# w_ada dot products spread differently over the weight chunks of the down products

## The chip, the core and the metric

The kernel runs on one core of a Trainium2 chip. The metric is the device time of one execution in microseconds. Before the change three runs took 2405.26, 2408.19 and 2410.62 us (median 2408.19). The core has a matmul engine (PE, with its weight loads shown as PEld), a vector engine (DVE), a scalar engine (ACT), GpSimd (POOL), and a queue on SyncE (SP) from which nearly all transfers are issued, one after the other.

## What is computed

Two layers of a streaming encoder over 512 positions and 1024 channels, in f32. Each layer is SwiGLU, mixer (two attentions, a pooling branch, a merge), SwiGLU. Every one of these three has a norm in front, and a shift, a scale and a gate that come from one vector `c`:

```python
c_act = jax.nn.silu(c)
for l in range(DEPTH):
    mod = (c_act @ w_ada[l] + b_ada[l]).reshape(B, N_MOD, D_MODEL)      # N_MOD = 9
    h = modulate(rms_norm(x, norm_gain[l, 0]), mod[:, 0], mod[:, 1])
    x = x + 0.5 * mod[:, 2][:, None, :] * swiglu(h, ffn_w_gate[l, 0], ffn_w_up[l, 0], ffn_w_down[l, 0])
    h = modulate(rms_norm(x, norm_gain[l, 1]), mod[:, 3], mod[:, 4])
    x = x + mod[:, 5][:, None, :] * hybrid_mixer(h, ...)
    h = modulate(rms_norm(x, norm_gain[l, 2]), mod[:, 6], mod[:, 7])
    x = x + 0.5 * mod[:, 8][:, None, :] * swiglu(h, ffn_w_gate[l, 1], ffn_w_up[l, 1], ffn_w_down[l, 1])
```

where `swiglu(h)` is `(silu(h @ w_gate) * (h @ w_up)) @ w_down`, 1024 to 2816 to 1024 channels. `c_act @ w_ada` is a product of one row with 75 MB of weights: 2 layers x 9 modulation rows x 8 blocks of 128 channels = 144 blocks of 512 KB.

## The kernel before

Channels lie on the partitions, so a modulation row is eight columns of 128 numbers. Each of the 144 blocks of `w_ada` is one *mod step* (`mod_step`, L200): one transfer of 512 KB (L203), one dot product with the broadcast `silu(c)` on DVE (L206), and for some rows a small operation behind it (L215, L217). The first 16 are done at the start. The other 128 stand in a list in the order in which they are needed (`mod_queue`), and `mod_pop` does the next one.

Who pops? `side_work` is called at every weight chunk (`wchunk`, L262): it adds `MOD_RATE[0]` to a credit and pops one step for each whole credit. And `mod_need(l, j)` pops whatever is still missing up to row `j` of layer `l`, all at once, at the place where a row must be complete.

A matmul weight chunk of 512 KB is loaded into one of two `raw` buffers (L266), split by ACT into a rounded high part `whi` (L277) and by DVE into the rest `wlo` (L279), and each product is three matmuls (L119 to L121: high x high, high x low, low x high). `whi` and `wlo` have three buffers each. In a down product, chunks arrive in a fixed order, and the last two of a pass are held and used together, one output tile after the other.

A SwiGLU (`Ffn.run`) works in three parts: 6, 8 and 8 tiles of 128 hidden channels. A part makes its tiles (gate and up), then multiplies them with their rows of `w_down` in two passes of 512 output channels. In part 0 the gate and up products are plain, in parts 1 and 2 they come from `seven` (L507), which makes two tiles at a time from seven half-size products, and `MOD_RATE` is 0 there. Part 0 also makes the operands for `seven` (`Blocks`) bit by bit on DVE and ACT.

The mod steps of a SwiGLU load into the four `v2` buffers. `seven` and `Blocks` use the same four: a mod transfer waits in the SP queue until its buffer is free, and everything behind it in that queue waits with it. In the last part's down products the norm of the next stage takes the `v2` or `b` buffers (`prefetch`), and the mod steps stop (`mod_tag` becomes "raw"). `prefetch` of a mixer first calls `mod_need(l, 5)`, ahead of the last part's first weight chunk. In the second half of a mixer 24 mod steps are done from `b` buffers, one a chunk.

The order of the instructions on each engine and in the SP queue is set at build time: a scheduler places them by its own estimate of when each could run, so transfers, dot products and splits may change places against the order of the code.

Of the kernel before, what the change touches and what calls it, by code (L numbers as in the profile page):

```python
# [40 lines left out]
def encoder_kernel(tc, xT, c, w_ada, b_ada, gains, w_gate, w_up, w_down, w_qkv, w_f, w_ubg,  # L41
# [28 lines left out]
    def mmt(shape=(P, T)):  # L70
        return ps.tile(list(shape), F32, tag="mm", bufs=4, name=nm("mm"))
# [17 lines left out]
    class Task:  # L89
# [3 lines left out]
        def run(self):  # L93
            fn, self.fn = self.fn, None
            if fn is not None:
                fn()

    def later(delay, fn, group=None):
        t = Task(pe[0] + delay, fn, group)
        tasks.append(t)  # L100
        return t
# [129 lines left out]
    def mod_need(l, j):  # L231
        while mod_ptr[0] < min(len(mod_queue), (l * 9 + j + 1) * 8 - 16):
            mod_pop()

    MOD_RATE = [1.0]
# [66 lines left out]
    def xd(d):  # L302
        return x_blocks[d // 2][:, d % 2, :]
# [84 lines left out]
    def k_outer(chunk_src, nch, lhs_rhs, before_last=None):  # L388

        if before_last is None:
            parts, nheld = [(None, slice(0, T), [acc() for _ in range(4)])], 2
        else:
            parts = [(hs, slice(hs * HALF, (hs + 1) * HALF), [b((P, HALF)) for _ in range(4)])
                     for hs, b in enumerate((mmt, acc))]
            nheld = 3

        def go(part, j, chunks):
            _, cols, accs = part  # L400
            for c, hi, lo in chunks:
                for kk in range(2):
                    a, b, x, y = lhs_rhs(hi[:, kk, :], lo[:, kk, :], 2 * c + kk, j)
                    triple(accs[j], a, b, x[:, cols], y[:, cols], start=(c == 0 and kk == 0),
                           stop=(c == nch - 1 and kk == 1))

        held = []
        for c in range(nch):
            if before_last is not None:
                if c == nch - 2:  # L410
                    quiet[0] = 8
                    before_last()
                quiet[0] = 8
            hi, lo = wchunk(chunk_src(c), (2, T))
            if c < nch - nheld:
                for part in parts:
                    for j in range(4):
                        go(part, j, [(c, hi, lo)])
            else:
                held.append((c, hi, lo))  # L420
        if before_last is not None:
            quiet[0] = 5
        for part in parts:
            for j in range(4):
                go(part, j, held[:-2])
            for j in range(4):
                go(part, j, held[-2:])
                yield j, part[0], part[2][j]

    def residual_tail(d, hs, acc_j, gate, nxt):  # L430

        cols = slice(0, T) if hs is None else slice(hs * HALF, (hs + 1) * HALF)
        x = xd(d)[:, cols]
        nc.vector.scalar_tensor_tensor(x, acc_j, gate, x, op0=ALU.mult, op1=ALU.add)  # L434
        if nxt is not None:
            nxt.norm.sq(d, hs)
            if d == KD - 1 and hs == 0:
                later(FRONT, lambda: nxt.norm.front(0, mmt))
                later(BACK, lambda: nxt.norm.back_start(0, mmt))
# [113 lines left out]
    def apply(parts, func, **kw):  # L553

        o = t1(T)
        n = T // len(parts)
        for i, p in enumerate(parts):
            nc.scalar.activation(o[:, i * n:(i + 1) * n], p, func, **kw)
        return o


    class Ffn:
# [32 lines left out]
        def run(self, nxt):  # L595
            l, s, ms = self.l, self.s, self.ms
            in_ffn[0] = True
            mod_tag[0] = "v2"
            parts = ((0, 6), (6, 8), (14, 8))
            for part, (f0, nf) in enumerate(parts):  # L600
                acts = []
                n = 0
                if part == 0 and self.norm is None:
                    acts = self.start()
                    n = 3
                    blocks = Blocks()
                elif part == 0:
                    g0, u0, g1 = self.pre
                    pg, pu, pg1 = mmt(), mmt(), mmt()
                    for hs in range(2):  # L610
                        self.norm.back(hs, acc if hs else mmt)
                        cols = slice(hs * HALF, (hs + 1) * HALF)
                        if hs == 0:
                            later(FRONT1, lambda: self.norm.front(1, acc))
                            later(BACK1, lambda: self.norm.back(1, acc))
                        for k in range(KD):
                            self.unit(pg, g0, cols, (k,))
                            self.unit(pu, u0, cols, (k,))
                        self.unit(pg1, g1, cols)
                    u1 = self.gate_up(1, 1)  # L620
                    acts.append(self.act(0, pg, pu))
                    pu1 = mmt()
                    self.unit(pu1, u1)
                    acts.append(self.act(1, pg1, pu1))
                    n = 2
                    blocks = Blocks(self.norm.xa, modc[:, l, 3 * ms])
                if part == 0:
                    blocks.schedule(T_FIRST, T_STEP)
                elif part == 1:
                    blocks.finish()  # L630
                MOD_RATE[0] = 0.0 if part else 1.0
                while part and n < nf:
                    both = [apply(p, AF.Silu)
                            for p in seven([w_gate[l, s, f0 + n + i] for i in range(2)], blocks, acc)]
                    ups = seven([w_up[l, s, f0 + n + i] for i in range(2)], blocks, mmt)
                    for i, sg in enumerate(both):
                        acts.append(self.act(n + i, None, ups[i], sg))
                    n += 2
                while n < nf:
                    g = self.gate_up(0, f0 + n)  # L640
                    u = self.gate_up(1, f0 + n)
                    pg, pu = mmt(), mmt()
                    self.unit(pg, g)
                    self.unit(pu, u)
                    acts.append(self.act(n, pg, pu))
                    n += 1
                mod_need(l, 3 * ms + 2)
                MOD_RATE[0] = 1.0
                for c0 in (0, T):
                    def src(c):  # L650
                        r0 = (f0 + 2 * c) * P
                        return w_down[l, s, r0:r0 + 2 * P, c0:c0 + T].rearrange("(k p) c -> p k c", p=P)

                    def ops(hi, lo, kt, j):
                        return (hi[:, j * P:(j + 1) * P], lo[:, j * P:(j + 1) * P],
                                acts[kt][:, 0, :], acts[kt][:, 1, :])

                    last = part == len(parts) - 1
                    if last and c0 == 0 and nxt is not None:
                        nxt.prefetch("v2")  # L660
                        mod_tag[0] = "raw"
                    split = last and c0 > 0
                    hook = None
                    if split:
                        hook = nxt.prefetch_weights if nxt is not None else (lambda: None)
                    for j, hs, o in k_outer(src, nf // 2, ops, hook):
                        d = c0 // P + j
                        residual_tail(d, hs, o, modc[:, l, 3 * ms + 2, d:d + 1], nxt if last else None)
                        if last and nxt is None:
                            cols = slice(0, T) if hs is None else slice(hs * HALF, (hs + 1) * HALF)  # L670
                            nc.sync.dma_start(out[:, d, cols], xd(d)[:, cols])
# [590 lines left out]
```

## Time and profile before

| what | us |
|---|---|
| median of 3 runs | 2408.19 |
| the profiled execution, its own time | 2409.17 |
| its span, first to last instruction | 2407.4 |
| first SwiGLU of layer 0 (`l, s` = 0, 0) | 0 to 371 |
| mixer of layer 0 | 371 to 861 |
| second SwiGLU of layer 0 (0, 1) | 861 to 1210 |
| first SwiGLU of layer 1 (1, 0) | 1210 to 1559 |
| mixer of layer 1 | 1559 to 2051 |
| second SwiGLU of layer 1 (1, 1) | 2051 to 2407 |

Matmuls are shown with a modelled duration and overlap, so the steady pace of a 128x512 matmul is read from start to start, not from its mean. Within the first SwiGLU, by the matmul lines: the down products of part 0 run from 92.6 to 125.3, those of part 1 from 205.4 to 249.0, and those of part 2 from 328.9 to 371.

The views used are the engines' busy time, the table by stretches of time with the clock granted to PE, the list of waits, the timeline of one engine, and the transfers with their time to landing.

### The profile page before, as it was taken

The page shows a single profiled execution, that of the slowest core. Times are in us where ns is not written, and L with a number is a line of the kernel's source. Part 1 is how long each engine was busy: PE and PEld are TensorE (multiplying, and loading weights), DVE is VectorE, ACT ScalarE, POOL GpSimd, SP SyncE. Part 2 cuts the span into 40 slices and gives each one's busy share as a digit, 9 for nine tenths or more (in the row PEclk, how much of TensorE's full clock was granted, in tenths as well). Part 3 has the DMA queues.
Part 4 walks back from the last instruction along what each step waited for, and adds up shares of the span by engine and source line. Part 5 has one row for each costly group of instructions (what it writes and reads, how often), then busy time and mean ns, then how long its engine had stood idle before and what let it go on. Part 6 is the DMA issues. An engine that isn't in the chain of part 4 may idle for free. (4 is left out here: it accounts for less than half of the span.)

```text
span 2407.4 us, 36815 instructions
## 1 busy us (share of the span) xinstructions
PE 2361.9 (98%) x14106; PEld 2086.8 (87%) x14106; DVE 1728.9 (72%) x3070; ACT 1197.8 (50%) x2090; POOL 351.7 (15%) x423
## 2 busy tenths in 40 slices
PE   7999999999999999999999999999999999999999
PEld 5898988778878898989998989888788788989898
DVE  8987886787665476878577868777866755658583
ACT  5353545786632353535543636466765324536352
POOL 3000011144432210000100000112444322000000
PEclk9999999999999999999999999999999999999999
DMA  7534362323345524343325343623233554223322
GB/s 274 201 106 175 106 219 88 93 79 107 109 171 200 175 99 156 108 165 105 132 87 185 105 165 104 215 83 102 74 120 104 198 182 168 71 97 106 101 95 103
DMA packets 116436, 320.93 MB, mean 133 GB/s; under 512 B 11138, under 2 KB 13314, under 8 KB 116260
## 3 DMA queue, kind: packets, MB, share of 16 engines
q1 hardware_dynamic: 115106, 314.38, 38.8%
q0 software_dynamic: 1152, 4.19, 0.5%
q8 instruction: 111, 1.82, 0.3%
q14 instruction: 65, 0.53, 0.1%
q10 hardware_dynamic: 2, 0.00, 0.0%
HBM read 312.16 MB, written 6.38 MB: 132 GB/s over the span
## 5 line engine op out<-in xcount | busy, mean ns | idle before, releaser
L277 ACT CAST whi<-raw 128x1024 fp32r<-128x1024 f32 (+1 forms) x267 | 277.5, 1043 | 449.6 <-PE acc L120 251.7
L279 DVE TENSOR_TENSOR wlo<-raw,whi 128x1024 fp32r<-128x1024 f32 x259 | 321.1, 1242 | 168.2 <-ACT whi L277 165.0
L119 PE MATMUL acc<-b,whi 128*128 128x512 f32 (+1 forms) x960 | 361.8, 377 | 3.8 <-ACT whi L277 3.8
L121 PE MATMUL acc<-b,wlo 128*128 128x512 f32 (+1 forms) x960 | 358.0, 373 | 0.6 <-DVE wlo L279 0.6
L120 PE MATMUL acc<-b,whi 128*128 128x512 f32 (+1 forms) x960 | 358.5, 373 | 0.0
L119 PEld LDWEIGHTS acc<-b,whi 128*128 128x128 f32 x960 | 181.4, 189 | 36.0 <-ACT whi L277 4.6
L121 PEld LDWEIGHTS acc<-b,wlo 128*128 128x128 f32 x960 | 181.7, 189 | 33.1 <-DVE wlo L279 1.5
L120 PEld LDWEIGHTS acc<-b,whi 128*128 128x128 f32 x960 | 181.8, 189 | 30.1
L119 PE MATMUL acc<-hhi,whi 128*128 128x512 f32 x480 | 191.3, 400 | 7.2 <-DVE b L1051 3.1
L120 PE MATMUL acc<-hlo,whi 128*128 128x512 f32 x480 | 188.0, 392 | 1.1 <-DVE hlo L711 1.1
L121 PE MATMUL acc<-hhi,wlo 128*128 128x512 f32 x480 | 187.7, 392 | 0.3 <-DVE wlo L279 0.3
L385 DVE TENSOR_TENSOR ptb<-v,ptb 128x1024 fp32r<-128x1024 f32 x128 | 156.5, 1223 | 36.4 <-ACT ptb L384 36.2
L384 ACT CAST ptb<-v 128x1024 fp32r<-128x1024 f32 x128 | 134.1, 1050 | 92.8 <-DVE v L452 47.9
L384 ACT CAST whi<-raw 128x1024 fp32r<-128x1024 f32 (+1 forms) x128 | 106.7, 833 | 99.3 <-PE acc L120 56.2
L119 PE MATMUL acc<-whi,hhi 128*128 128x512 f32 x336 | 137.8, 411 | 0.9 <-DVE xv L385 0.9
L206 DVE CUSTOM_DVE_ANT_0 v<-v,b,badac 128x1024 f32<-128x1024 f32 x96 | 127.2, 1333 | 12.3 <-DMA v<-in_w_ada_dram 12.0
L121 PE MATMUL acc<-whi,hlo 128*128 128x512 f32 x336 | 131.9, 393 | 0.0
L120 PE MATMUL acc<-wlo,hhi 128*128 128x512 f32 x336 | 131.7, 392 | 0.0
L385 DVE TENSOR_TENSOR wlo<-raw,whi 128x1024 fp32r<-128x1024 f32 (+1 forms) x128 | 121.7, 950 | 6.4 <-ACT whi L384 4.6
L434 DVE SCALAR_TENSOR_TENSOR xv<-acc,modc,xv 128x512 f32<-128x512 f32 (+1 forms) x112 | 77.2, 690 | 64.1 <-PE acc L121 64.1
L119 PEld LDWEIGHTS acc<-hhi,whi 128*128 128x128 f32 x480 | 90.7, 189 | 26.1 <-DVE b L1051 4.0
L329 POOL TENSOR_TENSOR ssum<-ssum,t 128x256 f32<-128x256 f32 (+1 forms) x45 | 46.9, 1043 | 442.4 <-ACT t L328 442.2
(315 smaller groups left out, 6664.5 us busy)
## 6 DMA issues: line engine op xcount, KB each, us to landing
v<-in_w_ada_dram SPq DMA_DIRECT2D x96, 512.0 KB, 5.0
raw<-in_w_down_dram SPq DMA_DIRECT2D x88, 512.0 KB, 3.7
raw<-in_w_up_dram SPq DMA_DIRECT2D x82, 512.0 KB, 3.6
raw<-in_w_gate_dram SPq DMA_DIRECT2D x79, 512.0 KB, 3.6
raw<-in_w_ubg_dram SPq DMA_DIRECT2D x56, 512.0 KB, 3.5
b<-in_w_ada_dram SPq DMA_DIRECT2D x48, 512.0 KB, 4.7
raw<-in_w_qkv_dram SPq DMA_DIRECT2D x42, 512.0 KB, 3.8
raw<-in_w_branch_dram SPq DMA_DIRECT2D x24, 512.0 KB, 3.7
```

The costliest lines, as they stand in the source:

```text
L119: mm(o, lh, rh, start=start, stop=False)
L120: mm(o, lh, rl, start=False, stop=False)
L121: mm(o, ll, rh, start=False, stop=stop)
L206: dot = nc.vector.tensor_tensor_reduce(out=raw, in0=raw, in1=silc[0], scale=1.0, scalar=badac[:, l, j, d:d + 1], op0=ALU.mult, op1=ALU.add ...
L277: nc.scalar.copy(hi, raw)
L279: lo_eng.tensor_tensor(lo, raw, hi.bitcast(F32), op=ALU.subtract)
L329: nc.gpsimd.tensor_tensor(self.ssum[:, cols], self.ssum[:, cols], q, op=ALU.add)
L384: nc.scalar.copy(hi, src)
L385: nc.vector.tensor_tensor(lo, src, hi.bitcast(F32), op=ALU.subtract)
L434: nc.vector.scalar_tensor_tensor(x, acc_j, gate, x, op0=ALU.mult, op1=ALU.add)
```

## The change

One number that was 1.0 for the down products of every part becomes 1.9, 1.2, 1.5 or 1.2, by layer and SwiGLU:

```diff
@@ -645,7 +645,7 @@
                     acts.append(self.act(n, pg, pu))
                     n += 1
                 mod_need(l, 3 * ms + 2)
-                MOD_RATE[0] = 1.0
+                MOD_RATE[0] = (1.9, 1.2, 1.5, 1.2)[2 * l + s]
                 for c0 in (0, T):
                     def src(c):
                         r0 = (f0 + 2 * c) * P
```

The mod steps are the same 128, in the same order; they are popped elsewhere. Steps by place, counted in the order in which the two programs pop them:

| place | before | changed |
|---|---|---|
| SwiGLU (0, 0), part 0, down, 6 chunks | 6 | 11 |
| SwiGLU (0, 0), part 1, down, 8 chunks | 8 | 15 |
| SwiGLU (0, 0), part 2, in one go by `mod_need(0, 5)` | 10 | 0 |
| SwiGLU (0, 1), down of parts 0 and 1 | 6 and 8 | 7 and 10 |
| SwiGLU (1, 0), part 0, in one go by `mod_need(1, 2)` | 2 | 0 |
| SwiGLU (1, 0), down of parts 0 and 1 | 6 and 8 | 9 and 12 |
| SwiGLU (1, 0), part 2, in one go by `mod_need(1, 5)` | 10 | 0 |
| SwiGLU (1, 1) | 0 | 0 |

The plain gate and up chunks of part 0 and the mixers keep their counts (the mixer of layer 0 does steps that stand two places later in the list).

First place: the SP queue at the start of the down products of part 2 of SwiGLU (0, 0). `raw` from `in_w_down_dram` are weight chunks, `v` from `in_w_ada_dram` mod steps, `b` from `in_w_qkv_dram` weights loaded ahead for the mixer. Before, the end of the nine steps ahead of the third chunk, and what follows:

```order
L203 DMA v2_502_3323<-in_w_ada_dram 128x1024
L203 DMA v2_503_3327<-in_w_ada_dram 128x1024
L203 DMA v2_504_3331<-in_w_ada_dram 128x1024
L266 DMA raw_517_3404<-in_w_down_dram 128x2x512
L203 DMA v2_505_3335<-in_w_ada_dram 128x1024
L266 DMA raw_520_3410<-in_w_down_dram 128x2x512
L266 DMA b_542_3552<-in_w_qkv_dram 128x2x512
L266 DMA raw_536_3492<-in_w_down_dram 128x2x512
```

Changed, from the first chunk on:

```order
L266 DMA raw_513_3350<-in_w_down_dram 128x2x512
L266 DMA raw_516_3380<-in_w_down_dram 128x2x512
L266 DMA raw_519_3410<-in_w_down_dram 128x2x512
L266 DMA raw_522_3416<-in_w_down_dram 128x2x512
L266 DMA b_544_3558<-in_w_qkv_dram 128x2x512
L266 DMA raw_538_3498<-in_w_down_dram 128x2x512
```

The third and fourth chunk now follow the first two with no mod step ahead of them.

Second place: DVE near the end of the down products of part 0 of the same SwiGLU. Rows `wlo` are splits of weight chunks (of the fourth, fifth and sixth chunk before; of the fifth and sixth in the changed program), `L206 ISA v` dot products, `xv` the residual sums of finished output tiles. Before:

```order
L279 TENSOR_TENSOR wlo_880<-raw_877,whi_879 128x1024
L434 TENSOR_SCALAR xv_78<-acc_753,modc,xv_78 128x512
L385 TENSOR_TENSOR b_884<-v_155_775,b_883 128x1024
L206 ISA v_176_911,modc<-v_176_911,b_73,badac 128x1024
L206 ISA modc 128x1
L434 TENSOR_SCALAR xv_78<-acc_754,modc,xv_78 128x512
L206 ISA v_180_920,modc<-v_180_920,b_73,badac 128x1024
L206 ISA modc 128x1
L434 TENSOR_SCALAR xv_85<-acc_755,modc,xv_85 128x512
L279 TENSOR_TENSOR wlo_917<-raw_914,whi_916 128x1024
L434 TENSOR_SCALAR xv_85<-acc_756,modc,xv_85 128x512
L279 TENSOR_TENSOR wlo_926<-raw_923,whi_925 128x1024
```

Changed, from the last residual sum on (three dot products stand between the fourth chunk's split and this piece already):

```order
L434 TENSOR_SCALAR xv_85<-acc_756,modc,xv_85 128x512
L206 ISA v_180_923,modc<-v_180_923,b_73,badac 128x1024
L206 ISA modc 128x1
L279 TENSOR_TENSOR wlo_930<-raw_927,whi_929 128x1024
L215 TENSOR_SCALAR apre<-modc,gainc 128x1
L206 ISA v_184_933,modc<-v_184_933,b_73,badac 128x1024
L206 ISA modc 128x1
L206 ISA v_185_937,modc<-v_185_937,b_73,badac 128x1024
L206 ISA modc 128x1
L215 TENSOR_SCALAR apre<-modc,gainc 128x1
L279 TENSOR_TENSOR wlo_944<-raw_941,whi_943 128x1024
```

Two dot products moved in between the splits of the fifth and the sixth chunk, which stood a single residual sum apart.

Third place: PE where it first uses that sixth chunk (`whi_182`, `wlo_183` before; `whi_187`, `wlo_188` changed). Before:

```order
L119 MATMUL acc_166_870<-b_128_657,whi_182_925 128x512
L120 MATMUL acc_166_870<-b_128_657,whi_182_925 128x512
L121 MATMUL acc_166_870<-b_128_657,wlo_183_926 128x512
L119 MATMUL acc_166_870<-b_144_742,whi_182_925 128x512
L120 MATMUL acc_166_870<-b_144_742,whi_182_925 128x512
L121 MATMUL acc_166_870<-b_144_742,wlo_183_926 128x512
```

Changed:

```order
L119 MATMUL acc_168_876<-b_128_657,whi_187_943 128x512
L120 MATMUL acc_168_876<-b_128_657,whi_187_943 128x512
L119 MATMUL acc_169_877<-b_98_493,whi_182_929 128x512
L120 MATMUL acc_169_877<-b_98_493,whi_182_929 128x512
L121 MATMUL acc_168_876<-b_128_657,wlo_188_944 128x512
L119 MATMUL acc_168_876<-b_144_742,whi_187_943 128x512
```

Two matmuls of the next output tile moved ahead of the first one that needs the sixth chunk's low part.

## The prediction, made before the changed kernel ran

> **What bounds the kernel now.** I read the engines' busy time first, then the table by stretches of time, then the idle gaps of PE with what ended them.
>
> ```profile
> PE 2361.9 (98%) x14106; PEld 2086.8 (87%) x14106; DVE 1728.9 (72%) x3070; ACT 1197.8 (50%) x2090; POOL 351.7 (15%) x423
> ```
>
> PE is busy for 98% of the span. The change takes no matmul away, so it can only gain where PE stands still or runs slowly, and can only lose by making PE wait. By stage (columns: length, then busy time of PE, PEld, DVE, ACT and POOL, granted clock, DMA share, GB/s):
>
> ```profile
> 0.00:371.00 371.00, 352.37 (x2216) 316.69 (x2217) 305.62 (x458) 179.28 (x277) 26.81 (x24) 1.00 0.52 178
> 861.00:1210.00 349.00, 349.00 (x2346) 323.56 (x2345) 260.41 (x408) 168.56 (x269) 9.30 (x9) 1.00 0.37 127
> 1210.00:1559.00 349.00, 346.37 (x2304) 319.70 (x2304) 273.75 (x430) 166.77 (x266) 10.74 (x11) 1.00 0.45 148
> ```
>
> SwiGLU (0, 1) has no idle PE time at all: there the new rate can gain nothing. SwiGLU (1, 0) has 349.00 - 346.37 = 2.63 us. In SwiGLU (0, 0) most of the idle time lies in the start, which the change leaves alone. The rest is in one place, and PE's timeline shows it together with that of (1, 0) (start, duration, what, and in brackets the idle time before and what ended it):
>
> ```profile
> 341.36 0.50 PE L119 MATMUL acc<-b,whi 128*128 128x512 f32 x1 [1.44 <-ACT whi L277]
> 342.62 0.50 PE L121 MATMUL acc<-b,wlo 128*128 128x512 f32 x1 [0.30 <-DVE wlo L279]
> ...
> 1529.63 0.50 PE L119 MATMUL acc<-b,whi 128*128 128x512 f32 x1 [2.33 <-ACT whi L277]
> 1530.89 0.74 PE L121 MATMUL acc<-b,wlo 128*128 128x512 f32 x1 [0.30 <-DVE wlo L279]
> ```
>
> Both stand at the third weight chunk of a last part's down products. Who made `whi` late is seen on ACT and in the SP queue:
>
> ```profile
> 318.10 15.54 SPq L203 DMA_DIRECT2D v<-in_w_ada_dram  x9
> 333.69 0.43 SPq L266 DMA_DIRECT2D raw<-in_w_down_dram  x1
> 340.26 1.04 ACT L277 CAST whi<-raw 128x1024 fp32r<-128x1024 f32 x1 [8.25 <-DMA raw<-in_w_down_dram]
> ...
> 1505.49 15.49 SPq L203 DMA_DIRECT2D v<-in_w_ada_dram  x9
> 1521.04 0.43 SPq L266 DMA_DIRECT2D raw<-in_w_down_dram  x1
> 1528.53 1.04 ACT L277 CAST whi<-raw 128x1024 fp32r<-128x1024 f32 x1 [9.17 <-DMA raw<-in_w_down_dram]
> ```
>
> Nine mod transfers occupy the queue for 15.5 us, since each waits for a `v2` buffer that a dot product must free, and the third chunk stands behind them. ACT had been idle for 8.25 and 9.17 us when it came. So the transfer, not ACT, is what is late.
>
> The gaps also cost something behind them. The same table in steps of 3.41 us:
>
> ```profile
> 339.72:343.14 3.42, 1.68 (x6) 0.97 (x6) 2.46 (x6) 1.28 (x2) 0.00 (x0) 1.00 0.95 373
> 343.14:346.55 3.41, 3.41 (x9) 2.67 (x9) 3.19 (x5) 1.86 (x2) 0.00 (x0) 0.50 0.75 247
> 1527.56:1530.97 3.41, 1.04 (x4) 0.57 (x4) 2.40 (x6) 1.04 (x1) 0.00 (x0) 1.00 0.82 317
> 1530.97:1534.39 3.42, 3.42 (x8) 2.67 (x9) 3.38 (x5) 2.09 (x2) 0.00 (x0) 0.50 0.64 196
> ...
> 1882.55:1885.96 3.41, 1.84 (x9) 1.25 (x8) 2.74 (x6) 2.14 (x4) 0.30 (x1) 1.00 0.00 0
> 1885.96:1889.40 3.44, 3.44 (x17) 2.83 (x16) 3.15 (x5) 0.51 (x1) 1.42 (x1) 1.00 0.39 141
> ```
>
> After each stall PE works through one step at a granted clock of 0.50, with 8 or 9 matmuls instead of 17. Idle times of 1.74 and 2.38 us within a step (3.42 - 1.68, 3.42 - 1.04) were followed by the half clock, 1.57 us (3.41 - 1.84) was not. One such step costs 3.41 x 0.5 = 1.71 us.
>
> **The change part by part.**
>
> *The two bursts of ten disappear.* The third chunk then follows the second in the SP queue and arrives with time to spare; next to be late would be the later chunks, which wait only for a `raw` buffer, as they do now without a stall. Gain: 1.44 + 0.30 + 1.71 = 3.45 us in (0, 0) and 2.33 + 0.30 + 1.71 = 4.34 us in (1, 0), together 7.79 us.
>
> [...]
>
> *The burst of two in (1, 0), part 0, disappears.* No PE wait stands at it; nothing is gained.
>
> *The dot products themselves* are the same 128. DVE and ACT gain or lose no work, only its place counts.
>
> *Part 0 of SwiGLU (0, 0): 11 steps instead of 6, among six chunks.* This stretch and its neighbours are the tightest, since DVE also makes operands for `seven`:
>
> ```profile
> 78.00:92.60 14.60, 14.60 (x66) 12.11 (x65) 13.72 (x21) 4.10 (x5) 0.00 (x0) 1.00 0.73 249
> 205.40:249.00 43.60, 43.60 (x195) 36.09 (x194) 27.69 (x41) 11.13 (x12) 0.00 (x0) 1.00 0.39 141
> ```
>
> Just ahead of it DVE works 94% of the time. The DVE rows that give each kind's price, from start to start:
>
> ```profile
> 85.77 1.28 DVE L206 CUSTOM_DVE_ANT_0 v<-v,b,badac 128x1024 f32<-128x1024 f32 x1
> 86.98 1.28 DVE L206 CUSTOM_DVE_ANT_0 v<-v,b,badac 128x1024 f32<-128x1024 f32 x1
> ...
> 97.82 1.22 DVE L385 TENSOR_TENSOR b<-v,b 128x1024 fp32r<-128x1024 f32 x1
> 98.95 0.68 DVE L452 TENSOR_TENSOR v<-v,v 128x512 f32<-128x512 f32 x1
> ...
> 108.73 1.23 DVE L279 TENSOR_TENSOR wlo<-raw,whi 128x1024 fp32r<-128x1024 f32 x1 [0.62 <-ACT whi L277]
> 109.87 0.74 DVE L434 SCALAR_TENSOR_TENSOR xv<-acc,modc,xv 128x512 f32<-128x512 f32 x1
> 110.54 1.21 DVE L279 TENSOR_TENSOR wlo<-raw,whi 128x1024 fp32r<-128x1024 f32 x1
> ```
>
> A dot product takes 1.21 us, a split 1.14 (L279) or 1.13 (L385), a residual sum 0.67, and I give L452 the same 0.67. From 98.95 to the end of the sixth chunk's split stand 3 dot products, 2 L452, 4 residual sums, one L385, 3 splits and small operations (0.2, my estimate): 3.63 + 1.34 + 2.68 + 1.13 + 3.42 + 0.2 = 12.4, so 111.4; the trace has 110.54 + 1.21 = 111.75, which bears the method out. The changed program has 8 dot products there: 18.45, so 117.4 if DVE never waits. When is that split needed?
>
> ```profile
> 114.43 0.39 PE L119 MATMUL acc<-b,whi 128*128 128x512 f32 x1
> 115.79 0.39 PE L119 MATMUL acc<-b,whi 128*128 128x512 f32 x1
> 116.25 0.39 PE L121 MATMUL acc<-b,wlo 128*128 128x512 f32 x1
> ```
>
> The sixth chunk's low part is first read at 116.25; a matmul takes (115.79 - 114.43) / 6 = 0.23 us, and two of them now stand ahead, so at 116.70. The old margin of 4.5 us becomes a lateness of 117.4 - 116.7 = 0.7 us at least. It is more if DVE has to wait for mod transfers, since eight dot products use four buffers twice. Their time from issue to landing, in three stretches (the last is a weight chunk among mod transfers):
>
> ```profile
> v<-in_w_ada_dram SPq DMA_DIRECT2D x2, 512.0 KB, 4.1
> v<-in_w_ada_dram SPq DMA_DIRECT2D x3, 512.0 KB, 5.3
> raw<-in_w_down_dram SPq DMA_DIRECT2D x2, 512.0 KB, 5.8
> ```
>
> With 4.1 us they arrive almost in step with DVE and the split is 0.8 us late; following the chain of buffer, transfer and dot product with 5.5 us it is 2.4 us late, with 6 us 3.8 us late. I take 1.7 us, between the first two, since the queue here is fuller than in the stretch that has 4.1. Ends: 0 (the order of arrival is kinder) and 3.8.
>
> *What follows it.* `seven` starts behind, and its second `raw` buffer is freed by the same late split:
>
> ```profile
> 115.99 0.69 DVE L515 TENSOR_TENSOR v<-raw 128x512 f32<-128x512 f32 x1 [4.25 <-DMA raw<-in_w_gate_dram]
> 120.80 1.23 DVE L385 TENSOR_TENSOR ptb<-v,ptb 128x1024 fp32r<-128x1024 f32 x1 [0.39 <-ACT ptb L384]
> ...
> 128.42 0.28 PE L130 MATMUL acc<-b,ptb 128*128 128x256 f32 x1
> ```
>
> Its first sum is ready 128.42 - 122.03 = 6.4 us early. The split ends 5.65 us later (117.4 for 111.75) and PE itself 0.7: 6.4 - 5.65 + 0.7 = 1.4 us remain. No cost; up to 1 us if the transfer lands late.
>
> *Part 1 of SwiGLU (0, 0): 15 instead of 8.* DVE is busy 27.69 of 43.60 us; seven more make 27.69 + 7 x 1.21 = 36.2, 83%. Where nine transfers held a chunk back by 15.5 us, now at most six stand ahead of one: about 15.54 / 9 x 6 = 10.4 us, 5.2 less than at the bursts, whose chunk was 1.44 and 2.33 us late. So it is some 3 us early. No cost.
>
> *SwiGLUs (0, 1) and (1, 0).* One to four more steps a part, 1.2 to 4.8 us of DVE time in 32.7 (6 chunks) or 43.6 us, where DVE stands at 260.41 / 349 = 75% and 78% on average and PE never waits in the parts concerned. No cost.
>
> *Sum.* 2409.17 (the profiled execution) - 7.79 + 1.7 = 2403.1. The median is 2408.19, 0.98 lower: **2402.1 us**.
>
> **The rivals.**
>
> 1. *No new wait in part 0.* If DVE has the split ready by 116.7, the whole gain stays: 2408.19 - 7.79 = 2400.4. For it: two matmuls were moved ahead to cover the split. Against: 0.7 us are missing even without a wait for a transfer.
>
> 2. *The new wait halves the clock.* If more than about 1.65 us of it fall into one step of 3.41 us (between the 1.57 and 1.74 above), 1.71 us are added. With 2.4 to 3.8 us of wait: 2400.4 + 2.4 + 1.7 = 2404.5 to 2400.4 + 3.8 + 1.7 = 2405.9. Landing times over 5.5 us decide it; the 5.8 us row speaks for it, the 4.1 row against.
>
> 3. *Slower: the mod transfers hold chunks back in every pass.* With two steps at a chunk, the SP queue gets two mod transfers ahead of each chunk. If a `v2` buffer came free more slowly than every 2.7 us (two in a chunk's 43.60 / 8 = 5.45 us), each of the four passes of parts 0 and 1 of SwiGLU (0, 0) would end in a stall like the bursts', 3.45 to 4.34 us: 2400.4 + 13.8 = 2414.2 to 2400.4 + 17.4 = 2417.8. For it: DVE's 94% ahead of part 0. Against: in the bursts one came free every 15.54 / 9 = 1.73 us.
>
> 4. *Half the gain is not there.* If the half clock were not due to the gaps, 4.37 - 1.7 = 2.7 us are gained: 2405.5. For it: the step after the 1.57 us kept its clock, so idle time does not always bring it. Against: twice out of twice over 1.74 us. [...]
>
> 5. *Nothing is gained at the former bursts*, because the third or a later chunk now waits for something else, say the weights loaded ahead for the mixer (`b` from `in_w_qkv_dram`), which share the queue: about 2408. For it: the DMA share of 0.95 in the stretch 339.72 to 343.14. Against: ten transfers fewer compete there.
>
> **How the numbers follow.** Forecast 0.50 (its own range 2400.5 to 2404), rival 1 0.13, rival 2 0.16, rival 3 0.10, rival 4 0.03, rival 5 0.08. A difference of 0.2%, 4.8 us, is about what a measurement of this kernel can tell from no change: faster is below 2403.4, slower above 2413.0. Faster: 0.42 of the forecast and rival 1, 0.55. Slower: rival 3 and a little of the others, 0.11. The same: 0.34. The range goes from 2399.5 (rival 1 less run-to-run spread) to 2408.5 (rival 5); it leaves out rival 3.
>
> **What would show it.** In the profile after: no gap over 0.3 us at the third chunk of either last part and no step at 0.50 behind it (rivals 4 and 5); SP sends that chunk right behind the second; a PE gap of about 1.7 us, ended by DVE's `wlo`, some 116 to 118 us after the start, at the full clock (rivals 1 and 2); parts 1 without gaps (rival 3); SwiGLU (0, 1) unchanged. The prediction is wrong if PE waits in part 1 or in the mixers, whose steps stand two places later in the list, or if the part 0 wait is over 4 us.

## The result: 2403.7 us, a little faster, and the profile after

The changed kernel takes 2403.7 us (median of 22 runs, 2401.71 to 2406.74), the kernel before 2407.55 (22 runs beside them, 2403.88 to 2411.23). The ratio is 0.9986, 95% interval 0.998 to 0.9993: 3.85 us or 0.14% faster. The interval leaves out a ratio of 1, yet the gain is less than the 0.2% that the prediction counts as a difference. The profiled execution has a span of 2403.0 us (2407.4 before).

The page's busy times, and then the same stages as before the change:

```profile
PE 2359.9 (98%) x14106; PEld 2085.6 (87%) x14106; DVE 1725.9 (72%) x3070; ACT 1198.4 (50%) x2090; POOL 351.7 (15%) x423
```
```profile
0.00:371.00 371.00, 353.31 (x2223) 317.18 (x2224) 306.56 (x464) 179.47 (x277) 26.84 (x24) 1.00 0.53 181
861.00:1210.00 349.00, 349.00 (x2345) 323.58 (x2345) 264.89 (x421) 168.70 (x269) 9.45 (x10) 1.00 0.39 132
```

SwiGLU (0, 1) still has no idle PE time. In the first SwiGLU idle time went away in one place and came up in another. The stretch of the down products of its last part, before and then after:

```profile
328.90:371.00 42.10, 40.36 (x235) 35.45 (x235) 28.57 (x44) 18.30 (x27) 8.70 (x8) 0.96 0.70 235
```
```profile
328.90:371.00 42.10, 42.10 (x268) 38.34 (x267) 19.83 (x27) 18.72 (x28) 8.44 (x8) 1.00 0.44 150
```

PE is busy from end to end, at the full clock, and the SP queue shows why: the four weight chunks stand there without a mod transfer among them, and the third chunk's split on ACT starts at 332.38 instead of 340.26, without a wait for its transfer (SP rows, then the ACT row, after the change):

```profile
318.19 9.43 SPq L266 DMA_DIRECT2D raw<-in_w_down_dram  x4
327.67 0.46 SPq L266 DMA_DIRECT2D b<-in_w_qkv_dram  x1
```
```profile
332.38 1.05 ACT L277 CAST whi<-raw 128x1024 fp32r<-128x1024 f32 x1
```

What came up is in part 0 of the same SwiGLU. PE's waits between 104 and 126 us (none there before the change), then PE's timeline around the longest one, then DVE:

```profile
PE acc L121 <- DVE wlo L279: 1.8, 2, 1.6
PE acc L119 <- DVE xv L434: 0.2, 1, 0.2
```
```profile
115.27 0.50 PE L121 MATMUL acc<-b,wlo 128*128 128x512 f32 x1 [0.23 <-DVE wlo L279]
...
116.99 0.39 PE L120 MATMUL acc<-b,whi 128*128 128x512 f32 x1
118.96 0.50 PE L121 MATMUL acc<-b,wlo 128*128 128x512 f32 x1 [1.58 <-DVE wlo L279]
119.30 0.39 PE L119 MATMUL acc<-b,whi 128*128 128x512 f32 x1
```
```profile
100.99 1.29 DVE L206 CUSTOM_DVE_ANT_0 v<-v,b,badac 128x1024 f32<-128x1024 f32 x1 [0.49 <-DMA v<-in_w_ada_dram]
...
107.92 1.29 DVE L206 CUSTOM_DVE_ANT_0 v<-v,b,badac 128x1024 f32<-128x1024 f32 x1 [0.77 <-DMA v<-in_w_ada_dram]
...
117.69 1.22 DVE L279 TENSOR_TENSOR wlo<-raw,whi 128x1024 fp32r<-128x1024 f32 x1
```

The split of the sixth chunk ends at 118.91 instead of 111.75, and PE waits for it. The wait costs more than its idle time: from 116.99 to 118.96 are 1.97 us where 0.23 is the pace, and the next matmul follows after 0.34 instead of 0.23, so 1.58 us of idle time cost 1.85 (1.97 + 0.34 for twice 0.23).

So the two traces are best compared from start to start: the 14106 matmuls stand in nearly the same order in both, so the start of the k-th in one minus its start in the other, taken at two places, tells what the stretch between them lost or gained. For the changed kernel:

| stretch (times before the change) | us |
|---|---|
| 92.6 to 160, down products of part 0 and the products behind | +3.58 |
| 160 to 328.9, part 1 and the products of part 2 | -0.06 |
| 328.9 to 371, third chunk of part 2, SwiGLU (0, 0) | -3.90 |
| 1310 to 1470, products of part 2, SwiGLU (1, 0) | +1.36 |
| 1470 to 1559, third chunk of part 2, SwiGLU (1, 0) | -4.80 |

Of the rest, the mixer of layer 1 (1559 to 2051) lost 1.36 us, and the other stretches gained 0.8 us and less. That mixer's loss differs between two executions of one and the same kernel (3.2 and 0.9 us with the short burst, below), so one pair of traces does not price it; what makes it differ was not looked into. The mixer of layer 0, whose steps stand two places later in the list, lost nothing (-0.57).

### The profile page after: what moved, and what is told of

The parts are those of the page before. It is cut to its first block, busy times and chain, and to the rows that moved or that the text cites. A ratio compares the mean times of both kernels' runs of the same rounds, so it can differ in the third digit from the quotient of the medians.

```text
span 2403.0 us, 36815 instructions
## 1 busy us (share of the span) xinstructions
PE 2359.9 (98%) x14106; PEld 2085.6 (87%) x14106; DVE 1725.9 (72%) x3070; ACT 1198.4 (50%) x2090; POOL 351.7 (15%) x423
## 5 line engine op out<-in xcount | busy, mean ns | idle before, releaser
L206 DVE CUSTOM_DVE_ANT_0 v<-v,b,badac 128x1024 f32<-128x1024 f32 x96 | 127.1, 1333 | 15.0 <-DMA v<-in_w_ada_dram 14.8
```

Of the source, the lines that this page charges most:

```text
L206: dot = nc.vector.tensor_tensor_reduce(out=raw, in0=raw, in1=silc[0], scale=1.0, scalar=badac[:, l, j, d:d + 1], op0=ALU.mult, op1=ALU.add ...
```

## The experiments

*Each half alone.* The rate of 1.9 in the first SwiGLU only:

```diff
-                MOD_RATE[0] = (1.9, 1.2, 1.5, 1.2)[2 * l + s]
+                MOD_RATE[0] = (1.9, 1.0, 1.0, 1.0)[2 * l + s]
```

> The new rate (1.9) in SwiGLU (0, 0) alone; 1.0 elsewhere, so the burst of ten in SwiGLU (1, 0) stays. Theory A (the two bursts and the wait in part 0 are separate, and their prices add): the stall at 340 us and the half clock behind it are gone, worth 3.7 us from start to start; PE waits for DVE's `wlo` in part 0 as in the changed kernel, costing 2.8 to 3.5; the stall at 1527 us stands. Time within 1 us of the kernel before. Theory B (the wait in part 0 is made up further on, since PE is not what ends the parts that follow): 3.7 us faster than before.

Measured: 2407.44 us beside 2407.77 for the kernel before, ratio 1.0001 (0.9992 to 1.001). By the trace, 92.6 to 160 lost 2.25 us and the third chunk gained 3.90; the products of part 2 lost another 1.5, where the changed kernel, which does the same steps there, lost nothing. PE's wait in part 0 was 1.4 us. So the first SwiGLU's half of the change gains nothing that these runs can tell (the interval runs from 1.9 us faster to 2.4 slower): in the trace part 0 alone gives back more than half of what the third chunk gains. Theory B, with 3.7 us, falls; theory A holds.

The other half, with 1.0 in the first SwiGLU (and 1.4 instead of 1.2 in (0, 1), so that the steps are done in time):

```diff
-                MOD_RATE[0] = (1.9, 1.2, 1.5, 1.2)[2 * l + s]
+                MOD_RATE[0] = (1.0, 1.4, 1.5, 1.2)[2 * l + s]
```

> The rate stays 1.0 in SwiGLU (0, 0), with its burst of ten; it is 1.4 in (0, 1) and 1.5 in (1, 0), so that (1, 0) has no burst. Theory A: stall and half clock at 1527 us are gone (4.5 us from start to start), those at 340 us stand, no wait in part 0. If the two waits of 0.4 us that the changed kernel has near 1454 and 1464 us come from the fuller down products of (1, 0), they are here too and 3.3 us are gained; if they are chance, they are not at that place and 4.5 are gained. Theory B gives 0 to 2 us: the sum of this one and of the rate in (0, 0) alone should be the 3.85 that the whole change gains.

Measured: 2405.44 beside 2407.77, ratio 0.9987 (0.9979 to 0.9996). Part 0 lost nothing, the third chunk of (1, 0) gained 4.81, and the waits near 1454 and 1464 were not there. The interval, 1 to 5 us of gain, does not choose between the two gains that were expected (3.3 and 4.5), and the median is below both. The two halves together (0.33 and 2.33 us by the medians) make 2.7 of the whole 3.85, within what such medians can tell.

A second thing was not expected. The stall at the third chunk of (0, 0) was there, and the half clock was not: that stretch was still 1.62 us shorter. In the trace before the change each of the two steps at half speed is 3.41 us long; they start at 343.14 and 1530.97, 1187.83 us apart, which is 348 times 3.4133 us, and the clock falls after the last matmul, at 2408.20, 257 such steps after the second start. With the rate in the first SwiGLU alone, the start of such a step at 1531.30 and the fall of the clock after the last matmul, at 2405.11, are 256 steps apart. Where an execution has no step at half speed I count the steps back from that fall, an estimate that rests on these distances. Here the clock falls at 2399.84, and so counted two steps start at 338.19 and 341.60, where before the change they start at 339.72 and 343.14. The start at 341.60 lies between the stall's two waits (PE timeline, then the table by such steps):

```profile
340.99 0.50 PE L119 MATMUL acc<-b,whi 128*128 128x512 f32 x1 [1.40 <-ACT whi L277]
...
342.25 0.51 PE L121 MATMUL acc<-b,wlo 128*128 128x512 f32 x1 [0.30 <-DVE wlo L279]
```
```profile
338.19:341.60 3.41, 2.01 (x10) 1.30 (x8) 1.69 (x5) 1.05 (x1) 0.00 (x0) 1.00 0.97 374
341.60:345.01 3.41, 3.11 (x14) 2.30 (x13) 3.38 (x6) 2.10 (x2) 0.00 (x0) 1.00 0.65 214
```

So one step at half speed costs about 3.90 - 2.28 = 1.62 us, where 2.28 is what the same stall cost here without it, and this execution did not pay it. Each run lists its mean granted clock, which one such step lowers to 0.9993 (1 - 0.5 x 3.41 / 2407): of 31 runs of the kernel before, 13 had 1.0 (mean 2406.33 us), 13 had 0.999 (2408.26) and 5 had 0.998 (2409.99), and the mean of all is 2407.73. All 33 runs of the changed kernel had 1.0. If the clock alone makes these groups differ, the half speed cost the kernel before 2407.73 - 2406.33 = 1.4 us on average; two further sets of its runs, worked out in the same way, give 0.7 and 1.7.

*How many steps part 0 bears.* Three kernels with other counts in parts 0 and 1 of the first SwiGLU (9 and 15, 13 and 12, 15 and 10 instead of 11 and 15; the first also has 1.4 instead of 1.2 in (0, 1)):

```diff
-                MOD_RATE[0] = (1.9, 1.2, 1.5, 1.2)[2 * l + s]
+                MOD_RATE[0] = ((1.5, 1.9), (1.4, 1.4), (1.5, 1.5), (1.2, 1.2))[2 * l + s][part] if part < 2 else 1.0
```
```diff
+                MOD_RATE[0] = ((2.3, 1.5), (1.2, 1.2), (1.5, 1.5), (1.2, 1.2))[2 * l + s][part] if part < 2 else 1.0
```
```diff
+                MOD_RATE[0] = ((2.6, 1.2), (1.2, 1.2), (1.5, 1.5), (1.2, 1.2))[2 * l + s][part] if part < 2 else 1.0
```

> As the changed kernel, with 9 steps in part 0 of SwiGLU (0, 0) instead of 11, and 15 in part 1 as before it (rates 1.5 and 1.9; 1.4 in SwiGLU (0, 1)). No burst is left. Theory A: the sixth chunk's split ends two dot products earlier, 2.4 us, and was 2.0 us too late: no wait in part 0 is left, or one under 0.3 us. 8.2 - 0.5 = 7.7 us faster than before, about 3 to 4 faster than the changed kernel. Rival: the wait comes from the transfers, which are still dense there, and half of it or more is left: 1.5 us faster than the changed kernel.

> As the changed kernel, with 13 steps in part 0 of SwiGLU (0, 0) (rate 2.3) and 12 in part 1 (rate 1.5). Theory A: each dot product more there delays the split by 1.2 to 1.35 us, so the wait grows from 1.6 to 4.0 to 4.3 us, over 1.7 us of it in one step of the clock, and a step at 0.50 follows: 2.5 + 1.7 = 4.2 us slower than the changed kernel, at about the time of the kernel before. Rival: the wait does not follow the count, since chunks and steps are spread anew by the scheduler: within 1 us of the changed kernel.

> As the kernel with 13 steps in part 0, with 15 (rate 2.6; 1.2 in part 1): a PE gap of 4.5 to 5.5 us in part 0. Theory on the clock (a step of 3.41 us of which PE is idle for more than half, 1.71 us, is followed by one at half speed; the gap of 2.83 us with 13 steps lay over the edge of two, 1.21 and 1.62): such a gap always fills more than half of a step, so at least one step at 0.50 follows it. 2 us of gap and 1.7 to 3.4 of clock: 3.5 to 5.5 us slower than with 13 steps, 2410 to 2412. Rival (a step must be idle from end to end): the half speed follows only where the gap covers a whole step, and is missing otherwise; 2408.5 then.

Measured, with the kernel before and the changed one (second row of the latter: the same kernel once more, below). The sets ran on different chips, so compare the last column:

| steps in part 0 | wait for `wlo`, us | lost from 92.6 to 160, us | median, us | median of the kernel before beside it | difference |
|---|---|---|---|---|---|
| 6 (before) | 0 | 0 | 2407.55 | | |
| 9 | 0 | 1.78 | 2402.05 | 2407.77 | -5.72 |
| 11 (changed) | 1.8 | 3.58 | 2403.7 | 2407.55 | -3.85 |
| 11 (again) | 1.8 | 3.39 | 2404.31 | 2407.41 | -3.10 |
| 13 | 2.8 | 5.58 | 2406.46 | 2407.77 | -1.31 |
| 15 | 2.7 | 7.02 | 2408.47 | 2406.86 | +1.61 |

The ratios to before are 0.9972 (0.9962 to 0.9982) with 9, 0.9992 (0.9983 to 1.0001) with 13 and 1.0006 (0.9997 to 1.0016) with 15. From 9 steps on the loss grows by 0.7 to 1 us a step (with 15, 1.6 us of it are a step at half speed). The wait for `wlo` does not: with 9 steps it is gone and with 15 it is shorter than with 13. What it does not take is lost behind it, at `seven`, whose transfers start when the last split frees a `raw` buffer (with 9 steps SP waits 6.2 us for that split). With 9 steps nearly all of the loss is there, at a wait for ACT, which stands with the split of a late up chunk ahead of the copy that PE needs. PE's waits between 104 and 140 us, then ACT:

```profile
PE acc L128 <- ACT v L542: 1.1, 1, 1.1
```
```profile
131.12 0.62 ACT L384 CAST whi<-raw 128x512 fp32r<-128x512 f32 x1 [3.74 <-DMA raw<-in_w_up_dram]
131.65 0.37 ACT L542 COPY v<-acc 128x256 f32<-128x256 f32 x1
```

Against the expectations: with 9 steps the wait went, as theory A had it, but the kernel is only 1.9 us faster than the changed one by the last column, nearer to the rival's 1.5 than to the 3 to 4 of theory A, because of the loss in `seven`. With 13 steps it is 2.5 us slower than the changed kernel, where 4.2 was expected, and with 15 steps 2.9 slower than with 13, where 3.5 to 5.5 was; the gaps of 4 and of 5 us did not come. The plain median with 15, 2408.47, is the one that the rival gave, but its trace speaks against the rival: the step behind the gap is at 0.50, although in the step with the gap PE was idle for 2.01 of 3.41 us and not from end to end (rows in the last section).

*Dot products or transfers?* Two kernels leave out one side of the 11 steps in part 0; first the dot products, cut to an eighth, then the transfers (`few[0]` is true in that part alone; `...` stands for lines left out here):

```diff
...
+            n = D // 8 if few[0] else D
-            dot = nc.vector.tensor_tensor_reduce(out=raw, in0=raw, in1=silc[0], scale=1.0,
+            dot = nc.vector.tensor_tensor_reduce(out=raw[:, :n], in0=raw[:, :n], in1=silc[0][:, :n], scale=1.0,
...
+                few[0] = (l, s, part) == (0, 0, 0)
```
```diff
...
+            n = D // 8 if few[0] else D
-            nc.sync.dma_start(raw, w_ada[l, j, d])
+            nc.sync.dma_start(raw[:, :n], w_ada[l, j, d][:, :n])
...
-            dot = nc.vector.tensor_tensor_reduce(out=raw, in0=raw, in1=silc[0], scale=1.0,
+            dot = nc.vector.tensor_tensor_reduce(out=raw, in0=silc[0] if few[0] else raw, in1=silc[0], scale=1.0,
...
+                few[0] = (l, s, part) == (0, 0, 0)
```

> The changed kernel, but the 11 dot products popped in part 0 of SwiGLU (0, 0) cover only the first 128 of 1024 columns (the sums of those modulation rows are left incomplete); their transfers are whole. Theory A (DVE's work makes the sixth chunk's split late): about 0.9 us less for each of eight dot products, 7 us, no wait for `wlo` in part 0; 2 us faster than the changed kernel. Rival (the transfers in the SP queue make it late): the wait stays at 1 us or more, now behind a late chunk.

> The changed kernel, but the 11 transfers of those steps bring only 128 of 1024 columns, and their dot products, whole as before, multiply the broadcast row with itself (those modulation rows are wrong numbers). Theory A: DVE no longer waits for steps' transfers (0.49 and 0.77 us behind 99 us in the changed kernel), so the split is 1.3 us earlier: the wait falls from 1.6 to 0.3 to 0.7 us, and does not go. Rival: the transfers are the cause, and the wait is gone (under 0.1 us).

Measured: 2401.53 and 2400.83 us beside 2406.86, both with ratio 0.9978 (0.9968 to 0.9988). Neither has a PE wait between 104 and 126 us; from 92.6 to 160 they lost 2.06 and 0.87 us. DVE in the first and in the second (their lines stand three further down, so L209 is the dot product and L282 the split):

```profile
104.84 0.35 DVE L209 CUSTOM_DVE_ANT_0 v<-v,b,badac 128x128 f32<-128x128 f32 x1 [1.99 <-DMA v<-in_w_ada_dram]
...
114.80 1.23 DVE L282 TENSOR_TENSOR wlo<-raw,whi 128x1024 fp32r<-128x1024 f32 x1 [2.06 <-ACT whi L280]
```
```profile
115.37 1.22 DVE L282 TENSOR_TENSOR wlo<-raw,whi 128x1024 fp32r<-128x1024 f32 x1
```

With short dot products DVE waits for the transfers all the more (1.99 us at one), and the last split for its own chunk by way of ACT (2.06); it ends at 116.03. With short transfers DVE never waits between 98 and 117 us and ends that split at 116.59, 2.3 us earlier than in the changed kernel. Both are just in time. So with either side cut down the split is ready when PE needs it, and only the two together make it late: the clean choice between them that the expectations offered was wrong. The 2.3 us are the waits for mod transfers that went: in the changed kernel two more of them stand ahead of the stretch shown, 0.53 us at 89.58 and 0.48 at 95.13, which with 0.49 and 0.77 make 2.27; the kernel with short transfers has none of the four.

*Is it the queue ahead of the third chunk?* All rates as before the change, but the mixer's prefetch asks for one row less, so the burst is two steps long:

```diff
-                MOD_RATE[0] = (1.9, 1.2, 1.5, 1.2)[2 * l + s]
+                MOD_RATE[0] = 1.0
...
-            mod_need(self.l, 5)
+            mod_need(self.l, 4)
```

> All rates 1.0 as before the change; but the mixer's prefetch asks for its rows 3 and 4 only, not for row 5, so its burst is 2 steps instead of 10, and the other 8 come up in the mixer (bursts of 2 to 4 stand at other places of the SwiGLUs behind). Theory A (the stall at the third chunk is the length of the queue ahead of it): eight steps of 1.73 us, 13.8 us, leave the queue ahead of it, so both stalls and their half clocks are gone, and no wait comes in part 0: 5.1 us of stalls from start to start and 1.4 of clock on average, 6.5 us faster than before, 2401.3, some 2.5 faster than the changed kernel. Rival (it is the dot products and the norm's work on DVE in the last part, which stay): half or less of that.

Measured: 2401.02 beside 2406.86, ratio 0.9971 (0.996 to 0.9982). The SP queue in the last part of (0, 0), and the stretch of its down products up to 366.60:

```profile
317.62 2.09 SPq L203 DMA_DIRECT2D v<-in_w_ada_dram  x2
321.97 2.12 SPq L266 DMA_DIRECT2D raw<-in_w_down_dram  x2
```
```profile
328.40:366.60 38.20, 38.20 (x235) 34.44 (x235) 17.88 (x22) 18.25 (x27) 8.43 (x8) 1.00 0.41 141
```

PE does the same 235 matmuls as in the 42.10 us before the change, without idle time, in 38.20. Third chunks: -3.90 and -4.80 us, as in the changed kernel; 92.6 to 160: 0.00. So the burst of ten makes the stalls; the norm's work on DVE, which stays, does not. The edit takes eight dot products away together with their transfers (22 DVE instructions in that stretch instead of 44), so it does not part the two. They hang together: before the change SP waited there for 8.3 us on DVE work of mod steps (L206, L215) and for 6.9 us on work with the products of `seven`, which hold the same buffers (L515, L558, L590). This one beats the kernel before, and on one chip also the changed kernel (below).

*Part 1 alone takes the surplus*, 6 and 18 steps; and the changed kernel and the short burst again, all three on one chip:

```diff
+                MOD_RATE[0] = ((1.0, 2.25), (1.4, 1.4), (1.5, 1.5), (1.2, 1.2))[2 * l + s][part] if part < 2 else 1.0
```

> As the kernel with 9 and 15 steps, with 6 steps in part 0 of SwiGLU (0, 0), as before the change, and 18 in part 1 (rates 1.0 and 2.25). Theory A (only part 0 is too tight for more; part 1 has room): from the start to part 1's gate and up products the trace runs as before the change, at no loss (with 9 steps it lost 1.8 us, with 11 2.3 to 3.6), both stalls are gone, and part 1, with 27.69 + 10 x 1.21 = 39.8 of 43.6 us of DVE work, shows at most 0.5 us of waits: 2401.0, as the kernel with the short burst. Rival (part 1 fills up as part 0 did): waits for `wlo` of 1 to 3 us there, 2402 to 2404.

> The changed kernel once more, beside the two others. If the two waits of 0.4 us at 1454 and 1464 us belong to the change, they are here again; if they are chance (the same two stood near 2336 and 2347 before the change, near 1123 and 1134 in another run), they are elsewhere or missing. The wait in part 0 is 1.4 to 1.8 us again and costs 2.2 to 3.6 up to part 1's products; no step at half speed; 2403.5 to 2404.5.

> The kernel with the short burst once more, for its time beside the changed kernel's on one chip: 2400.5 to 2401.5, 2.5 to 3.5 below the changed kernel; no wait in part 0, no stall at the third chunks.

Measured beside 2407.41: 2402.45 (ratio 0.9975, 0.9967 to 0.9984), 2404.31 (0.9987, 0.9978 to 0.9997) and 2400.99 (0.9972, 0.9962 to 0.9982). With 18 steps part 1 lost 0.52 us and the products of part 2 0.75; part 0 lost nothing. No wait for `wlo` stands in part 1, so the rival's mechanism did not come, though the time lies in its range (2402 to 2404) and 1.5 us above theory A's. In the profiled execution 1.1 us were lost at a pair of waits near 1125 and 1135, of the kind that the next sentence is about. The like pair at 1454 and 1464 us did not come back in the changed kernel, so its 1.36 us there were chance: another stood near 1130 and 1141 in the kernel with 15 steps, where the changed kernel had none. What sets it off is not known. The short burst is 3.3 us faster than the change on the same chip.

## Why the prediction was right, and where its terms were not

The forecast was 2402.1 us, and the time of 2403.7 lies in the range and in the forecast's own range (2400.5 to 2404). Its mechanism happened step by step, but three of its sizes were off. The gain was to be 6.1 us and was 3.85: about 2.0 too much was put down to the clock and 1.8 too little to part 0, against 1.1 too little to the stalls. That the time came within 1.6 us is in part luck: the median of three runs from which the forecast starts lies 0.6 us above that of the 22 runs. And the time is not below 2403.4, where the prediction lets "faster" begin; it falls under "the same", which had 0.34.

- *The two bursts of ten disappear.* Right: no wait and no step at 0.50 is left at either third chunk.
- *4.37 us of stalls* (the idle times of 1.44, 0.30, 2.33 and 0.30 us) were too few. From start to start the one in (0, 0) was 3.90 - 1.62 = 2.28 us for 1.74 of idle time, and the one in (1, 0) about 4.80 - 1.62 = 3.2 for 2.63. The step that failed is reading a stall's price from its idle time: each stall is two waits, and with the 0.27 us that a wait in part 0 cost beyond its idle time (last section) they come to 1.74 + 0.54 = 2.28 and 2.63 + 0.54 = 3.17. Together 5.5.
- *3.42 us of clock* were too many. I took the two steps at half speed of one profiled execution for a property of the kernel. Of 31 runs of the kernel before, 13 list a clock of 1.0, and on average such steps cost 1.4 us (0.7 to 1.7), an estimate from the listed clocks. I had two rows of a single execution and did not ask how the steps lie in another. The sum even goes from that execution to the median, 0.98 us lower, and leaves the term whole. It is the largest error.
- *1.7 us in part 0* was right as a wait (1.8) and wrong as a price: 3.58 and 3.39 us in two executions of the changed kernel, 2.25 in the one with the rate in the first SwiGLU alone. The walk itself held: without a wait I had 117.4 for the end of the split, the trace has 118.91, and 1.26 us of the difference are the two waits for transfers (0.49 and 0.77). The price has three parts. The long wait cost 1.85 us. Two short ones, which the prediction did not have, show 0.18 and 0.23 us of idle time (at 112.94 for a residual sum, at 115.27 for the fifth chunk's split) and cost 0.45 and 0.49. And *what follows it*, left at no cost, took about 0.7 in `seven`, within the 1 us given as its bound.
- With measured sizes: 5.5 + 1.4 - 3.5 = 3.4 us of gain, and with the bounds 2.7 (0.7 of clock, 3.5 in part 0) to 5.0 (1.7, 2.25). Measured: 3.85.
- *Burst of two, part 1, SwiGLUs (0, 1) and (1, 0)*: no cost, as forecast. (0, 1) has no idle PE time, 160 to 328.9 lost nothing, and the 1.36 us in (1, 0) did not come back.
- *Rival 1* (no new wait) and *rival 3* (chunks held back in every pass) did not happen. *Rival 5* did not: behind the third chunk PE is busy to the end of the stretch, 42.10 of 42.10 us.
- *Rival 2* (the new wait halves the clock) did not happen in 33 runs: in the profiled execution 1.58 us of idle time fell into one step of 3.41 us and the next was at 1.00, where 1.72 was followed by 0.50 elsewhere (below). With 13 steps 2 of 10 runs list a mean clock under 1.0, with 15 steps 7 of 10.
- *Rival 4* did not happen: the half speed went with the gaps. Before the change the two steps at 0.50 stand right behind steps with 1.74 and 2.38 us of idle PE time, and 18 of 31 runs list a clock under 1.0; in the changed kernel neither third chunk has a wait or a step at 0.50, and all 33 runs list 1.0. That less than 7.79 us can be had came true for another reason.

## What to carry to other kernels

A burst of small jobs ahead of a transfer in one queue can be shortened in two ways, by doing the jobs earlier or by not asking for those that nobody needs yet; the second left every tight place as it was and was worth 3.3 us more than the first on the same chip. Work moved to "earlier" has to be priced at the place where it lands, by the chain of buffer, transfer and vector work there, and then at the next user of the buffers that this chain frees. And an effect that one profiled execution shows must be weighed by how many runs have it: here that execution had two steps at half speed, while 13 of 31 runs of the same kernel list a clock of 1.0.

## What the runs showed of the hardware that I had not expected

In three of the profiled executions PE's granted clock was 0.50 for one step of 3.41 us behind a step in which PE was idle for 1.72 to 2.38 us. Two of these steps are those before the change, with 1.74 and 2.38 us. The table by steps, the step with the idle time and the one behind it: with the rate in the first SwiGLU alone, with 15 steps in part 0, in the changed kernel, with 13 steps, with the short burst, and with the short burst again.

```profile
1527.88:1531.30 3.42, 1.70 (x6) 1.13 (x7) 2.01 (x2) 1.31 (x2) 0.00 (x0) 1.00 0.87 340
1531.30:1534.71 3.41, 3.41 (x10) 2.64 (x9) 2.93 (x5) 1.74 (x2) 0.00 (x0) 0.50 0.85 268
```
```profile
116.92:120.33 3.41, 1.40 (x6) 1.18 (x7) 3.23 (x7) 0.00 (x0) 0.00 (x0) 1.00 0.92 293
120.33:123.75 3.42, 3.42 (x10) 2.64 (x9) 3.25 (x7) 0.21 (x1) 0.00 (x0) 0.50 0.54 188
```
```profile
115.92:119.33 3.41, 1.83 (x9) 1.19 (x8) 3.06 (x7) 0.45 (x1) 0.00 (x0) 1.00 0.56 154
119.33:122.75 3.42, 3.42 (x17) 2.81 (x16) 2.21 (x3) 0.60 (x1) 0.00 (x0) 1.00 0.55 153
```
```profile
117.03:120.44 3.41, 1.80 (x8) 1.48 (x9) 3.41 (x8) 0.00 (x0) 0.00 (x0) 1.00 0.30 80
120.44:123.85 3.41, 3.41 (x17) 2.71 (x16) 2.59 (x6) 1.05 (x1) 0.00 (x0) 1.00 0.39 139
```
```profile
1902.95:1906.36 3.41, 1.64 (x7) 1.38 (x8) 3.41 (x5) 0.24 (x1) 1.02 (x1) 1.00 0.03 10
1906.36:1909.78 3.42, 3.42 (x17) 2.84 (x16) 0.04 (x1) 0.00 (x0) 1.19 (x1) 1.00 1.02 403
```
```profile
688.51:691.92 3.41, 1.72 (x8) 1.08 (x7) 2.28 (x7) 1.54 (x3) 0.90 (x1) 1.00 0.00 0
691.92:695.33 3.41, 3.41 (x16) 2.82 (x15) 3.35 (x4) 1.11 (x3) 0.79 (x1) 1.00 0.22 56
```

Idle times of 1.72, 1.74, 2.01 and 2.38 us in a step were followed by half speed; 1.58, 1.61, 1.69 and one of 1.77 were not. So the idle PE time that the profile shows does not part the two groups: 1.72 stands in the first and 1.77 in the second. Nor does the weight loads' busy time (second number): 1.18 us of it was followed by half speed with 15 steps, and 1.08 was not in the last pair. What parts them was not shown. With 13 steps the gap was 2.83 us long, 1.21 of it in the step ahead of the pair above and 1.61 in the pair's first step, and no step at 0.50 followed in the profiled execution; with 15 it was 2.70, of which 2.01 lay in one step, and one followed.

The second is the price of a restart. In the changed kernel's part 0 the three waits of PE's 128x512 matmuls, with 0.18, 0.23 and 1.58 us of idle time, cost 0.45, 0.49 and 1.85 us, so 0.26 to 0.27 more than the profile shows: 0.16 lies in the record of the matmul ahead (0.39 us long at a pace of 0.23), 0.11 in the step from the matmul behind the wait to the next (0.34 for 0.23). With 0.27 us for each wait, the prices of the three waits in part 0 and of the two stalls come out to within 0.02 us.
